# A two-layer hybrid trunk on one Trainium2 core: one block of scores for both key triangles of sliding attention, and running sums by four products

## The chip, the cores and the metric

The kernel runs on one core of a Trainium2 chip. The metric is the device time of one execution in microseconds (us), and lower is better. A core has five engines that matter here: TensorE (PE in the profile; its weight loads are PEld), VectorE (DVE), ScalarE (ACT), GpSimd (POOL) and SyncE (SP). Each works through its own instructions in the order in which the program holds them, and waits for others through semaphores. On-chip data lies in SBUF, products of TensorE in PSUM, inputs and outputs in DRAM.

## What is computed

Two layers, each applied to a stream of 256 tokens of width 1024. A layer projects the normalised stream by one large matrix, feeds three token mixers (a state-space scan called SSD, sliding-window attention, and "forgetting" attention with a decay bias), gates and projects each, merges them, projects once more and adds to the stream. The parts that the change touches are these, cut from the reference:

```
# sliding attention: 16 heads of 64, 4 key/value heads, window 128, blocks of 128 queries
scores = einsum(qb, kb) * 64**-0.5                  # kb: the block before and the own block, 256 keys
diff = qi + 128 - sj                                # 0 <= diff < 128 is inside the window
scores = where(0 <= diff < 128 and key_pos >= 0, scores, -inf)
probs = softmax(concat([scores, sink]))[..., :-1]   # the sink takes a share and has no value
y = einsum(probs, vb) * silu(z)
# forgetting attention
log_f = log_sigmoid(f_logit + f_bias);  cum = cumsum(log_f, axis=1)      # over all 256 tokens
sc = sc + cum[query] - cum[key]
# SSD: decays inside a chunk of 128 tokens
a_cum = cumsum(dt * a)                              # per chunk;  decay = exp(a_cum[l] - a_cum[s])
```

For the second block of queries, the inside of the window is a triangle of the previous block's keys (key index above the query's) and the complementary triangle of the own block's keys (key index at or below the query's). Together they have 128 keys per query.

## The kernel before

**Dense work and weights.** All weights come from DRAM in parts of 512 KB (`load_part`, issued on SP's queue). Each part is split into two: `hi`, a copy on ScalarE (L291), and `lo`, the rest, on VectorE (L292, `lo = raw - hi`). A dense product takes three products, hi by hi and two with a `lo`. Six buffers hold raw parts and six hold split parts; a split buffer is released when TensorE has used it.

**The order of TensorE's work** is written by a planner while the program is built. `mm` and `transpose` (L100 to L110) put an instruction on TensorE and move a planned clock on. The mixers are generators: one is `launch`ed, and when it yields a number (the constants D_..., L25 to L27) it is asked again once the planned clock has moved on by so many microseconds. `pump` (L147) enters those that are due after each dense unit. So TensorE's order is fixed by hand, and dense products lie between the steps of a mixer. The orders of VectorE, ScalarE and GpSimd are set by the tile scheduler when the program is built.

**PSUM** has eight banks of 128 by 512: `pmm` gives three in turn to dense products, `pmx` gives five in turn to everything else. A bank that is given out again is written only after its last reader is done.

**Sliding attention** takes four heads at a time (a "quad", four quads per layer; `swa_quad` and `attn_quad`, L587 to L687). A quad takes four `pmx` banks for the scores of its four heads: 128 columns for the first block of queries (own keys) and 256 for the second (previous and own keys). TensorE fills them by 32 products. VectorE adds the mask and takes the row minimum (L615, once per block and head: 128 and 256 wide, into SBUF), ScalarE takes the exponential with its row sum (L621), a few small operations add the sink's share (L625 to L628), then come a reciprocal (L630) and eight scalings (L633). After D_SOFT = 7 planned microseconds TensorE transposes twelve 128 by 128 blocks (L647) in two halves, D_SOFT2 = 3 apart; ScalarE copies the three resulting banks to SBUF (L652). After D_EVAC = 3 come the products with the values. Two quads' values are taken together, at the start of a later quad (L676: gate times product, on VectorE, straight from PSUM). `attn_quad` also serves forgetting attention.

**Running sums** (`decay_logits`, L714 to L763): from 32 logits per token a chain of small VectorE operations makes the rates of the SSD (`da`) and of the forgetting (`lf`). D_CUM = 12 planned microseconds after that, TensorE makes the sums by products with a triangle of ones: two into a bank `pa` (tokens on the partitions, evicted to `acum`), two into a bank `pr` (heads on the partitions, SSD) and three into a bank `pf` (heads on the partitions, forgetting). `pr` and `pf` go through ScalarE to one SBUF tile and by one DMA to DRAM (`cumd`, L763), from where each group of SSD heads (L808) and each pair of forgetting heads (L985) reads its rows, copied to all 128 partitions.

In TensorE's order the sums of a layer stand after the scores of its third sliding quad. Of the five `pmx` banks, four are then that quad's scores; `pa` takes the fifth, `pr` the bank of its first head, `pf` the bank of its second.

Of the kernel before, what the change touches and what calls it, by code (L numbers as in the profile page):

```python
# [16 lines left out]
P = 128  # L17
# [30 lines left out]
def hybrid_trunk(  # L48
# [29 lines left out]
    def pmx():  # L78
        return PS("mx", 5)
# [105 lines left out]
    for j in range(2):  # L185
# [16 lines left out]

    wmask = T("wmask", [P, 2 * P])
    nc.gpsimd.memset(wmask, 0.0)
    nc.gpsimd.affine_select(out=wmask[:, P:2 * P], in_=wmask[:, P:2 * P],
                            compare_op=ALU.is_ge, fill=NEG, base=0,
                            pattern=[[-1, P]], channel_multiplier=1)
    nc.gpsimd.affine_select(out=wmask[:, 0:P], in_=wmask[:, 0:P],
                            compare_op=ALU.is_ge, fill=NEG, base=-1,
                            pattern=[[1, P]], channel_multiplier=-1)  # L210
    mhalf = T("mhalf", [P, 8])
# [374 lines left out]

    def attn_quad(y, last, products, biases, nsink, v, vcols, sz, gated, scored=lambda: None):  # L587

# [18 lines left out]
        products(score)  # L607
        for p in range(2):
            pp = pps[p]
            ps_ = slice(4 * p, 4 * p + 4)  # L610
            ns = None if nsink is None else nsink(p)
            for i in range(2):
                for b, sl in blocks:
                    e = 4 * p + 2 * i + b
                    nc.vector.tensor_tensor_reduce(  # L615
                        out=pp[:, i, sl], in0=score(p, i, b), in1=biases(p, i, b), scale=-0.125,
                        scalar=1.0e30 if ns is None else ns[:, i:i + 1],
                        op0=ALU.add, op1=ALU.min, accum_out=nm[:, e:e + 1])
                for b, sl in blocks:
                    e = 4 * p + 2 * i + b  # L620
                    act(pp[:, i, sl], pp[:, i, sl], AF.Exp, scale=-1.0, bias=nm[:, e:e + 1],  # L621
                        accum_out=sums[:, e:e + 1])
            if nsink is not None:
                es = T("es", [P, 4], bufs=2)
                tt(es.rearrange("p (i b) -> p i b", i=2), nm[:, ps_].rearrange("p (i b) -> p i b", i=2),  # L625
                   bc(ns, 2, 2), op=ALU.subtract)
                act(es, es, AF.Exp)
                tt(sums[:, ps_], sums[:, ps_], es, op=ALU.add)  # L628
            rs = T("rsum", [P, 4], bufs=4)
            nc.vector.reciprocal(rs, sums[:, ps_])  # L630
            for i in range(2):
                for b, sl in blocks:
                    ts(pp[:, i, sl], pp[:, i, sl], rs[:, 2 * i + b:2 * i + b + 1], 0.5,  # L633
                       op0=ALU.mult, op1=ALU.mult)
        yield D_SOFT
        scored()

        order = [(0, 0), (0, 1), (1, 0), (1, 1), (0, 2), (1, 2),
                 (2, 0), (2, 1), (2, 2), (3, 0), (3, 1), (3, 2)]
        at = {hb: (n // 4, n % 4 * P) for n, hb in enumerate(order)}  # L640
        pTs = []
        for n, (h, b) in enumerate(order):
            if n == 6:
                yield D_SOFT2
            if n % 4 == 0:
                pt = pmx()
            transpose(pt[:, n % 4 * P:(n % 4 + 1) * P], pps[h // 2][:, h % 2, b * P:(b + 1) * P], ident)  # L647
            if n % 4 == 3:
                if n == 3:
                    two = T("L4", [P, 2, 512])  # L650
                pT = T("L2", [P, 512]) if n == 11 else two[:, n // 4, :]
                act(pT, pt, AF.Copy)  # L652
                pTs.append(pT)
        yield D_EVAC
        tokens["pp"] += 1

        def products_with_values(bank):
            py = bank()
            for p in range(2):
                for b, o in ((0, 0), (1, P)):  # L660
                    for i in range(2):
                        n, c = at[2 * p + i, 2 * b]
                        mm(py[64 * i:64 * i + 64, S * p + o:S * p + S], v[:, b, vcols(p, i)],
                           pTs[n][:, c:c + S - o], start=(b == 0), stop=(b == 1))
            return py
# [3 lines left out]
        if len(pair) == 2:  # L669
# [3 lines left out]
            def values():  # L673
                for py, (_, _, own) in zip([f(bank) for (_, f, _), bank in zip(quads, (pmx, pmm))], quads):
                    o = own()
                    tt(o, py.rearrange("p (u s) -> p u s", u=2), o, op=ALU.mult)  # L676
            if not last:
# [8 lines left out]
    def swa_quad(y, g, q):  # L686
        yield lambda: 1 in y.sz  # L687

        def products(score):
# [7 lines left out]
        yield from attn_quad(  # L697
            y, g == 3, products, lambda p, i, b: wmask[:, P:2 * P] if b == 0 else wmask,
            lambda p: y.nsink[:, 4 * g + 2 * p:4 * g + 2 * p + 2], y.bv,
            lambda p, i: slice(64 * g, 64 * g + 64),  # L700
            lambda: y.sz[1][:, 2 * g:2 * g + 2, :], lambda: (1, 2 * g + 1) in y.zdone)

# [11 lines left out]
    def decay_logits(y):  # L714
# [20 lines left out]
        y.dt = T("dt", [P, 2, 16])  # L735
        lf = T("lf", [P, 2, 16])
        ts(w[:, :, 0:16], u[:, :, 0:16], 0.0, 0.5, op0=ALU.max, op1=ALU.mult)
# [3 lines left out]
        tt(lf, w[:, :, 16:32], q3[:, :, 16:32], op=ALU.subtract)  # L741
        ts(lf, lf, 2.0, None, op0=ALU.mult)
        da = T("da", [P, 2, 16])
        tt(da, y.dt, bc(y.nega, 1, 2), op=ALU.mult)
# [7 lines left out]
        cum = T("L2", [16, 2, S])  # L752
# [225 lines left out]
    def fox_quad(y, j):  # L978
# [535 lines left out]
```

## Time and profile before

| | us |
|---|---|
| median of 3 runs | 820.61 (819.9 to 821.44) |
| the profiled execution | 820.72 |
| its span in the trace | 819.0 |
| PE busy in it | 808.4 |
| DVE busy | 671.5 |
| ACT busy | 547.6 |
| POOL busy | 172.6 |

The profiled execution's time is 1.72 us above its span: that much lies around the first and last instruction that the trace shows. A page of the profile gives busy times of the engines, the granted TensorE clock (PEclk), a chain of waits that ended last, and groups of instructions by source line. A timeline row gives start, duration, engine, line, operation, output and inputs, shape and count. Most durations overlap the next instruction's start, since engines are pipelined: what an instruction costs its engine's queue is the distance from its start to the next one's.

### The profile page before, as it was taken

How to read it: one execution, taken by the hardware profiler on the slowest of the kernel's cores; microseconds unless marked ns; L12 is line 12 of the kernel's file. 1: busy time of each engine (PE TensorE's matmuls, PEld its weight loads, DVE VectorE, ACT ScalarE, POOL GpSimd, SP SyncE). 2: the span in 40 equal slices, each digit the busy share in tenths (PEclk: the TensorE clock that was granted, in tenths of full speed). 3: DMA queues.
4: the chain of work that ended last, by engine and by line, in shares of the span. 5: the costliest groups of instructions: out<-in, count | busy, mean ns of one | idle time of the engine just before them, and what ended most of it. 6: DMA issues, size and time to landing. Idle time of an engine off the chain costs nothing.

```text
span 819.0 us, 15070 instructions
## 1 busy us (share of the span) xinstructions
PE 808.4 (99%) x5242; PEld 721.2 (88%) x5242; DVE 671.5 (82%) x1468; ACT 547.6 (67%) x1186; POOL 172.6 (21%) x232
## 2 busy tenths in 40 slices
PE   8999999999999999999999999999999999999996
PEld 8998988888888988888999898889888889888896
DVE  6879899888998787965786989988899878787665
ACT  7777878775776767543666777886567767684452
POOL 3066113130210001030005621314004210102100
PEclk9999999999999999999999999999999999999999
DMA  9897869797865554866689787869868565467632
GB/s 312 278 261 193 211 187 256 190 233 214 232 206 157 180 168 148 276 208 205 221 265 265 186 222 206 228 179 259 243 206 231 155 181 163 137 208 265 206 104 77
DMA packets 141653, 170.35 MB, mean 208 GB/s; under 512 B 9314, under 2 KB 110298, under 8 KB 141578
## 3 DMA queue, kind: packets, MB, share of 16 engines
q1 hardware_dynamic: 114960, 140.53, 54.8%
q0 software_dynamic: 12928, 12.63, 9.5%
q10 hardware_dynamic: 13690, 16.24, 6.5%
q8 instruction: 41, 0.67, 0.3%
q14 instruction: 34, 0.28, 0.1%
HBM read 154.63 MB, written 2.16 MB: 191 GB/s over the span
## 4 chain that ended last, share of the span: by engine, by line
PE 85%; DVE 4%; DMA 4%; ACT 4%; issue 2%; POOL 0%; SPq 0%; ACTq 0%; DVEq 0%; POOLq 0%
PE mm L106 75%; PE mx L106 7%; PE mx L110 3%; DMA L<-cumd 2%; DVE lo L292 1%; ACT hi L291 1%; DVE L L781 1%; ACT pp L621 1%; DMA L<-L 1%; DMA raw<-in_w_in_dram 1%; DMA bias<-cumd 1%; ACT L L778 0%; ACT L L490 0%; DVE L L830 0%; POOL bias L991 0%
## 5 line engine op out<-in xcount | busy, mean ns | idle before, releaser
L292 DVE TENSOR_TENSOR lo<-raw,hi 128x1024 fp32r<-128x1024 f32 (+2 forms) x276 | 310.5, 1144 | 53.2 <-ACT hi L291 50.5
L106 PE MATMUL mm<-L,hi 128*128 128x512 f32 x1056 | 353.2, 386 | 0.0
L106 PE MATMUL mm<-hi,L 128*128 128x512 f32 (+2 forms) x1232 | 323.3, 351 | 0.1
L291 ACT ACTIVATE hi<-raw 128x1024 fp32r<-128x1024 f32 (+2 forms) x276 | 263.9, 981 | 57.2 <-PE mm L106 45.2
L106 PE MATMUL mm<-L,lo 128*128 128x256 f32 x1056 | 266.6, 273 | 0.0
L106 PEld LDWEIGHTS mm<-hi,L 128*128 128x128 f32 x1232 | 216.9, 190 | 24.1 <-issue 1.3
L106 PEld LDWEIGHTS mm<-L,hi 128*128 128x128 f32 x1056 | 194.5, 190 | 26.4 <-issue 3.2
L106 PE MATMUL mm<-lo,L 128*128 128x512 f32 (+2 forms) x616 | 213.8, 349 | 1.8 <-DVE lo L292 1.8
L106 PEld LDWEIGHTS mm<-L,lo 128*128 128x128 f32 x1056 | 202.1, 191 | 5.5
L106 PEld LDWEIGHTS mm<-lo,L 128*128 128x128 f32 x616 | 116.3, 190 | 14.1 <-DVE lo L292 2.6
L492 POOL DMA_DIRECT2D L<-L x68 | 59.4, 925 | 184.5 <-ACT L L491 151.3
L621 ACT ACTIVATE pp<-pp,nm 128x128 f32<-128x128 f32 (+1 forms) x128 | 56.5, 442 | 30.8 <-DVE nm L615 30.7
L991 POOL TENSOR_SCALAR_AFFINE_SELECT bias<-bias 128x128 f32<-128x128 f32 x64 | 34.6, 592 | 93.5 <-DMA bias<-cumd 92.7
L781 DVE SCALAR_TENSOR_TENSOR L<-L,vec,L 128x255 f32<-128x255 f32 (+2 forms) x96 | 46.2, 481 | 2.2 <-ACT L L778 0.5
L490 ACT ACTIVATE L<-mm 128x256 f32<-128x256 f32 x84 | 31.6, 376 | 15.9 <-PE mm L106 14.2
L1025 ACT ACTIVATE L<-L 128x512 f32<-128x512 f32 x24 | 15.1, 629 | 31.6 <-DVE L L1022 27.2
L633 DVE TENSOR_SCALAR pp<-pp,rsum 128x128 f32<-128x128 f32 (+1 forms) x128 | 32.5, 319 | 0.5
L492 POOL DMA_DIRECT2D qt<-L x16 | 14.5, 990 | 81.9 <-ACT qt L491 40.4
L877 DVE SCALAR_TENSOR_TENSOR L<-L,L 128x256 f32<-128x256 f32 x48 | 21.4, 449 | 8.6 <-ACT L L876 8.3
L652 ACT ACTIVATE L<-mx 128x512 f32<-128x512 f32 x48 | 26.8, 595 | 1.5 <-PE mx L110 1.5
L1070 POOL TENSOR_TENSOR L<-L,L 128x512 f32<-128x512 f32 x8 | 12.8, 1598 | 68.4 <-DVE L L1069 68.4
L912 POOL TENSOR_TENSOR sm<-sm,mhalf 128x4 f32<-128x4 f32 x8 | 8.1, 1019 | 90.5 <-DVE sm L909 90.5
(197 smaller groups left out, 841.8 us busy)
## 6 DMA issues: line engine op xcount, KB each, us to landing
raw<-in_w_in_dram SPq DMA_DIRECT2D x191, 512.0 KB, 4.7
raw<-in_w_proj_dram SPq DMA_DIRECT2D x48, 512.0 KB, 5.3
L<-L POOLq DMA_DIRECT2D x72, 128.0 KB, 5.0
raw<-in_w_out_dram SPq DMA_DIRECT2D x16, 512.0 KB, 5.1
bias<-cumd ACTq DMA_DIRECT2D x16, 256.0 KB, 3.4
L<-cumd ACTq DMA_DIRECT2D x8, 512.0 KB, 5.9
L<-in_gate_bias_dram ACTq DMA_DIRECT2D x12, 256.0 KB, 5.9
qt<-L POOLq DMA_DIRECT2D x16, 128.0 KB, 5.6
```

The lines of the kernel that those rows point to most:

```text
L106: nc.tensor.matmul(o, a, b, **kw)
L110: nc.tensor.transpose(o, a, i)
L291: keep(act)(hi, src, AF.Copy)
L292: keep(tt)(lo, src, hi.bitcast(F32), op=ALU.subtract)
L490: act(halves(lo), ordered(p[:, S:2 * S]), AF.Copy)
L492: nc.gpsimd.dma_start(out, lo, accum_op=ALU.add)
L621: act(pp[:, i, sl], pp[:, i, sl], AF.Exp, scale=-1.0, bias=nm[:, e:e + 1], accum_out=sums[:, e:e + 1])
L633: ts(pp[:, i, sl], pp[:, i, sl], rs[:, 2 * i + b:2 * i + b + 1], 0.5, op0=ALU.mult, op1=ALU.mult)
L652: act(pT, pt, AF.Copy)
L781: stt(a[:, s:S], x_[:, 0:S - s], y.vec[:, 16 * j + u:16 * j + u + 1], a[:, s:S], op0=ALU.mult, op1=ALU.add)
L877: stt(o, th, 1.0, o, op0=ALU.add, op1=ALU.mult)
L991: nc.gpsimd.affine_select(out=bias[:, i, dst], in_=bias[:, i, src], compare_op=ALU.is_ge, fill=NEG, base=0, pattern=[[-1, P]], channel_mul ...
```

## The change

Sliding attention (`window=True`) and the running sums are rewritten; forgetting attention keeps its code.

- **One block of scores.** The first block of queries is treated as before. In the second block, the previous block's scores are copied over the own block's scores wherever the own ones are masked, by a predicated copy inside PSUM, once per head. The 128 wide result gets its row maximum by a reduction, a small operation per two heads makes the bias, and ScalarE's exponential reads PSUM itself, 128 wide in place of 256.
- **Normalisation** by two operations per quad (128 by 512, reciprocals broadcast) in place of eight scalings. The factor 0.5 goes to the gate's operation after the values.
- **Transposes.** Eight per quad in place of twelve. The first half's bank is copied by ScalarE; the second half's bank is taken twice by VectorE, times the mask `other` and times the triangle `tri`, to part the two triangles again. The first half is asked for after D_FOLD = 8 in place of D_SOFT = 7.
- **Running sums.** Both rates share a tile; `pa` takes one product, and a bank `pc` takes three (two chunks in column groups, with 32 columns for both rates, and one that adds the first chunk's total to the forgetting sums). One copy of 64 by 128 goes to SBUF and two DMAs write `cumd`, now `[2, 16, 256]`, so that the later readers' rows lie side by side. D_CUM is 17 in place of 12.

```
-D_GN1, D_GN2, D_CUM, D_H, D_M = 8.0, 13.5, 12.0, (4.8, 6.4), 5.0
+D_GN1, D_GN2, D_CUM, D_H, D_M = 8.0, 13.5, 17.0, (4.8, 6.4), 5.0
+D_FOLD = 8.0
...
+        def chances(h, b, of):
+            e = 4 * b + h
+            act(pps[b][:, h // 2, h % 2 * P:h % 2 * P + P], of, AF.Exp, scale=0.125 if b else -1.0,
+                bias=nm[:, e:e + 1], accum_out=sums[:, e:e + 1])
+
+        for h in range(4) if window else ():
+            own = pps[0][:, h // 2, h % 2 * P:h % 2 * P + P]
+            nc.vector.tensor_tensor_reduce(
+                out=own, in0=scs[h][:, 0:P], in1=wmask, scale=-0.125, scalar=nsink[:, h:h + 1],
+                op0=ALU.add, op1=ALU.min, accum_out=nm[:, h:h + 1])
+            chances(h, 0, own)
+        for h in range(4) if window else ():
+            own = scs[h][:, 2 * P:3 * P]
+            nc.vector.copy_predicated(own, wmask.bitcast(mybir.dt.uint32), scs[h][:, P:2 * P])
+            nc.vector.tensor_reduce(nm[:, 4 + h:5 + h], own, axis=mybir.AxisListType.X, op=ALU.max)
+            if h % 2 == 1:
+                hs = slice(h - 1, h + 1)
+                nh = slice(3 + h, 5 + h)
+                stt(nm[:, nh], nm[:, nh], -0.125, nsink[:, hs], op0=ALU.mult, op1=ALU.min)
+                for i in (h - 1, h):
+                    chances(i, 1, scs[i][:, 2 * P:3 * P])
+        for b in range(2) if window else ():
+            ...
+            nc.vector.reciprocal(rs, sums[:, hs])
+            tt(of_heads(b), of_heads(b), bc(rs.rearrange("p (i j) -> p i j", i=2), 3, P), op=ALU.mult)
...
-        yield D_SOFT
+        yield D_FOLD if window else D_SOFT
...
+                for h in range(4):
+                    transpose(pt[:, h * P:(h + 1) * P], pps[b][:, h // 2, h % 2 * P:h % 2 * P + P], ident)
+                ptv = pt.rearrange("p (h q) -> p h q", h=4)
+                if b == 0:
+                    act(first[:, 0, :], pt, AF.Copy)
+                else:
+                    tt(first[:, 1, :].rearrange("p (h q) -> p h q", h=4), ptv, bc(other, 1, 4), op=ALU.mult)
+                    tt(both.rearrange("p (h q) -> p h q", h=4), ptv, bc(tri, 1, 4), op=ALU.mult)
...
+                    if window:
+                        stt(o, po, 0.5, o, op0=ALU.mult, op1=ALU.mult)
...
         yield D_CUM
         pa = pmx()
-        for c in range(2):
-            mm(pa[:, 16 * c:16 * c + 16], tri, da[:, c, :], start=True, stop=True)
+        mm(pa[:, 0:32], tri, rates[:, :, 1, :], start=True, stop=True)
...
-        pr = pmx()
+        pc = pmx()
         for c in range(2):
-            mm(pr[0:16, c * P:(c + 1) * P], da[:, c, :], tri, start=True, stop=True)
-        act(cum[:, 0, :], pr[0:16, 0:S], AF.Copy)
-        pf = pmx()
-        mm(pf[0:16, 0:P], lf[:, 0, :], tri, start=True, stop=True)
-        mm(pf[0:16, P:S], lf[:, 0, :], ones, start=True, stop=False)
-        mm(pf[0:16, P:S], lf[:, 1, :], tri, start=False, stop=True)
-        act(cum[:, 1, :], pf[0:16, 0:S], AF.Copy, scale=-8.0)
-        y.cumd = dr.tile([16, 2, S], F32, name=f"cumd{y.l}", tag=f"cumd{y.l}")
-        nc.scalar.dma_start(y.cumd, cum)
+            mm(pc[32 - 32 * c:64 - 32 * c, 0:P], rates[:, c, :, :].rearrange("p w c -> p (w c)"), tri,
+               start=True, stop=(c == 0))
+        mm(pc[0:16, 0:P], rates[:, 0, 0, :], ones, start=False, stop=True)
+        cum = T("L1", [64, P])
+        act(cum, pc[0:64, 0:P], AF.Copy)
+        y.cumd = dr.tile([2, 16, S], F32, name=f"cumd{y.l}", tag=f"cumd{y.l}")
+        for c in range(2):
+            nc.scalar.dma_start(y.cumd[:, :, c * P:(c + 1) * P].rearrange("w c s -> (w c) s"),
+                                cum[32 - 32 * c:64 - 32 * c, :])
...
-        nc.scalar.dma_start(bcg, y.cumd[4 * g:4 * g + 4, 0, :].partition_broadcast(P))
+        nc.scalar.dma_start(bcg, y.cumd[1, 4 * g:4 * g + 4, :].partition_broadcast(P))
...
-                                y.cumd[2 * (j + p):2 * (j + p) + 2, 1, :].partition_broadcast(P))
+                                y.cumd[0, 2 * (j + p):2 * (j + p) + 2, :].partition_broadcast(P))
```

In the changed program, too, a layer's sums stand after the scores of the third sliding quad, sixteen dense instructions behind them; `pa` has the fifth bank and `pc` the bank of that quad's first head, whose second block ScalarE's exponential now reads.

More of the change, by code (lines that the diff above doesn't have):

```diff
@@ L585, in u_bq, with attn_quad @@
         return rotated(y, done)
-    def attn_quad(y, last, products, biases, nsink, v, vcols, sz, gated, scored=lambda: None):
+    def attn_quad(y, last, products, biases, nsink, v, vcols, sz, gated, scored=lambda: None, window=False):
         yield Half("pp")
@@ L607, in attn_quad, with of_heads @@
         products(score)
-        for p in range(2):
+        def of_heads(b):
+            return pps[b].rearrange("p i (j q) -> p i j q", j=3)[:, :, 0:2, :]
+        def chances(h, b, of):
[19 more added lines that the diff above has]
+        for b in range(2) if window else ():
+            hs = slice(4 * b, 4 * b + 4)
+            es = T("es", [P, 4], bufs=2)
+            tt(es, nm[:, hs], nsink, op=ALU.subtract)
+            act(es, es, AF.Exp)
+            tt(sums[:, hs], sums[:, hs], es, op=ALU.add)
+            rs = T("rsum", [P, 4], bufs=4)
+            nc.vector.reciprocal(rs, sums[:, hs])
+            tt(of_heads(b), of_heads(b), bc(rs.rearrange("p (i j) -> p i j", i=2), 3, P), op=ALU.mult)
+        for p in () if window else range(2):
             pp = pps[p]
             ps_ = slice(4 * p, 4 * p + 4)
-            ns = None if nsink is None else nsink(p)
             for i in range(2):
@@ L661, in products_with_values @@
                     for i in range(2):
[L662 to L664 removed]
+                        h = 2 * p + i
+                        if window:
+                            m = both[:, h * P:(h + 1) * P] if b else first[:, :, h * P:(h + 1) * P]
+                        else:
+                            n, c = at[h, 2 * b]
+                            m = pTs[n][:, c:c + S - o]
+                        mm(py[64 * i:64 * i + 64, S * p + o:S * p + S], v[:, b, vcols(p, i)], m,
+                           start=(b == 0), stop=(b == 1))
             return py
@@ L697, in swa_quad @@
         yield from attn_quad(
-            y, g == 3, products, lambda p, i, b: wmask[:, P:2 * P] if b == 0 else wmask,
-            lambda p: y.nsink[:, 4 * g + 2 * p:4 * g + 2 * p + 2], y.bv,
+            y, g == 3, products, None, y.nsink[:, 4 * g:4 * g + 4], y.bv,
             lambda p, i: slice(64 * g, 64 * g + 64),
-            lambda: y.sz[1][:, 2 * g:2 * g + 2, :], lambda: (1, 2 * g + 1) in y.zdone)
+            lambda: y.sz[1][:, 2 * g:2 * g + 2, :], lambda: (1, 2 * g + 1) in y.zdone, window=True)
     def logits(y, t, i, p):
```

69 lines of the change are left out of this document (35 added, 34 removed).

## The prediction

> **What bounds the kernel now.** I read the page first: busy times, granted clock and the chain that ended last.
>
> ```profile
> span 819.0 us, 15070 instructions
> PE 808.4 (99%) x5242; PEld 721.2 (88%) x5242; DVE 671.5 (82%) x1468; ACT 547.6 (67%) x1186; POOL 172.6 (21%) x232
> PEclk9999999999999999999999999999999999999999
> PE 85%; DVE 4%; DMA 4%; ACT 4%; issue 2%; POOL 0%; SPq 0%; ACTq 0%; DVEq 0%; POOLq 0%
> ```
>
> TensorE is busy for 99% of the span at the full clock, and 85% of the chain is its own. VectorE at 82% is next. Then the waits of PE (total, times, longest), and the two stretches that hold the sliding quads, one per layer (length, busy time of PE, PEld, DVE, ACT, POOL, clock, DMA share):
>
> ```profile
> PE mm L106 <- DVE lo L292: 1.8, 2, 1.2
> 66.00:160.00 94.00, 94.00 (x723) 84.02 (x722) 86.19 (x236) 75.89 (x202) 27.65 (x34) 1.00 0.75 200
> 457.00:552.00 95.00, 94.82 (x726) 84.51 (x726) 86.50 (x237) 75.93 (x202) 27.50 (x34) 1.00 0.74 199
> ```
>
> In both stretches PE has no idle time worth a name, and DVE is busy for 86.2 of 94 and 86.5 of 95 us, 91 to 92%. So an instruction taken from PE saves its time, as long as PE then waits for nobody; but DVE, which the change touches most, has only some 8 us of slack in 94. Over the whole kernel PE waits 1.8 us for late `lo` parts, in two waits.
>
> **Work taken from PE.** The chain of waits through layer 0's quads (start, length, what) gives the price of one instruction:
>
> ```profile
> 75.97 0.66 PE mx L110 x6
> 112.53 1.52 PE mx L106 x32
> 114.06 2.82 PE mm L106 x16
> 116.88 1.54 PE mx L106 x14
> ```
>
> Six transposes take 0.66 us, 0.11 each. The change drops 4 of 12 per quad, 8 quads: 32 x 0.11 = 3.5 us. The seven products of the running sums (14 records, two passes each) take 1.54 us, 0.22 each; four remain, so 3 x 0.22 x 2 layers = 1.3 us. **PE's own work: -4.8 us.** The score products, the products with values and all dense work stay.
>
> **A wait that goes.** In layer 1 the old sums already waited a little:
>
> ```profile
> 116.71 0.51 PE L106 MATMUL mx<-da,tri 128*128 128x16 f32 x4
> 117.16 0.61 PE L106 MATMUL mx<-tri,da 128*16 128x128 f32 x4
> 507.97 0.52 PE L106 MATMUL mx<-da,tri 128*128 128x16 f32 x4
> 508.60 0.61 PE L106 MATMUL mx<-tri,da 128*16 128x128 f32 x4
> 509.28 0.39 PE L106 MATMUL mx<-tri,lf 128*16 128x128 f32 x2
> ```
>
> `pa` to `pr` is 0.45 us in layer 0 and 0.63 in layer 1, `pr` to `pf` 0.68 where four records at 0.11 need 0.44. That is about 0.4 us of waiting for the banks of the quad's heads. Those products go: **-0.4**. What is late next is the following term.
>
> **A wait that comes: `pc` on the bank of the third quad's first head.** `pr` got that bank when VectorE had read it (L615 writes to SBUF, so its last reader is the second L615 row of that head). Now the bank is held through predicated copy, reduction, the small operation for two heads, and ScalarE's exponential, which reads PSUM. PE stands still at `pc`, and all dense work queues behind it. So I compare two arrival times in layer 0.
>
> *PE at `pc`.* Counted with the prices above through the changed order, the third quad's scores come 1.7 us later than now (more dense work and the later D_FOLD lie ahead; fewer transposes). They end at 112.53 + 1.52 + 1.7 = 115.75. Then stand sixteen dense instructions (2.82) and `pa` (0.22): PE is at `pc` at 118.8.
>
> *VectorE at the quad.* Its timeline now:
>
> ```profile
> 102.47 2.36 DVE L292 TENSOR_TENSOR lo<-raw,hi 128x1024 fp32r<-128x1024 f32 x2 [0.75 <-ACT hi L291]
> 104.75 0.48 DVE L781 SCALAR_TENSOR_TENSOR L<-L,vec,L 128x255 f32<-128x255 f32 x1
> 105.14 0.17 DVE L709 TENSOR_TENSOR u<-mm,hb 128x16 f32<-128x16 f32 x1
> ...
> 114.01 0.68 DVE L676 TENSOR_TENSOR L<-mx,L 128x512 f32<-128x512 f32 x1
> 114.61 0.21 DVE L733 SCALAR_TENSOR_TENSOR L<-L 128x64 f32<-128x64 f32 x1
> ...
> 116.01 0.34 DVE L615 CUSTOM_DVE_ANT_0 pp<-mx,wmask,nsink 128x128 f32<-128x128 f32 x1
> 116.28 0.48 DVE L615 CUSTOM_DVE_ANT_0 pp<-mx,wmask,nsink 128x256 f32<-128x256 f32 x1
> 116.68 0.35 DVE L615 CUSTOM_DVE_ANT_0 pp<-mx,wmask,nsink 128x128 f32<-128x128 f32 x1
> ```
>
> The last idle time is the 0.75 us ahead of 102.47. From there the queue runs without a gap for 13.54 us to the quad's first row at 116.01, although the scores were there at 114.05: DVE is already 1.95 us behind. That stretch, from the same `lo` to the same row, holds 5 `lo`, 6 filter taps (L781) and the sums' chain. In the changed order it holds 7 `lo`, 9 taps, and the two new mask products of the second quad. A `lo` takes 2.36/2 = 1.14 to 1.18 of the queue, a tap 0.39 (104.75 to 105.14), a 128 by 512 product from PSUM 0.60 (114.01 to 114.61): 2 x 1.14 + 3 x 0.39 + 2 x 0.60 = 4.7 us more, 18.2 in all. Because less lies ahead on DVE and PE, I let the stretch start 0.3 to 1.6 us sooner; the quad's first row is then at 102.47 - 0.3 (1.6) + 18.2 = 120.4 (119.1).
>
> *Time to free the bank.* Behind that first row DVE's order has three more 128 wide mins, three predicated copies, three reductions and the small operation before head 0's exponential. A min takes 0.27 of the queue (116.01 to 116.28). No row shows the predicated copy or a 128 wide reduction. From below stand a small reduction and an all-SBUF operation of 128, from above the min at twice the width:
>
> ```profile
> L246 DVE TENSOR_REDUCE sm<-ss 128x1 f32<-128x2 f32 x4 | 0.6, 148 | 0.8 <-ACT L L242 0.8
> 179.47 2.19 DVE L830 SCALAR_TENSOR_TENSOR L<-L,acum,negtri 128x128 f32<-128x128 f32 x8
> L621 ACT ACTIVATE pp<-pp,nm 128x128 f32<-128x128 f32 x64 | 24.9, 390 | 30.5 <-DVE nm L615 30.5
> ```
>
> That is 0.15 to 0.40 for a reduction and 0.27 (2.19/8) to 0.40 for a copy; I take 0.25 and 0.27, those of like width. Then 4 x 0.27 + 3 x 0.27 + 3 x 0.25 + 0.1 = 2.75 us (2.4 to 3.5). The exponential takes 0.39, and two hand-overs between engines some 0.25. The bank is free 3.4 us after the first row, at 122.5 to 123.8, and PE has waited since 118.8: **3.7 to 5.0, I take 4.3 us in layer 0.** In layer 1 the queue is further behind:
>
> ```profile
> 503.73 1.59 PE L106 MATMUL mx<-L,qt 32*128 32x128 f32 x32
> 507.79 0.34 DVE L615 CUSTOM_DVE_ANT_0 pp<-mx,wmask,nsink 128x128 f32<-128x128 f32 x1
> ```
>
> Scores from 503.73 end by 505.25, the first row is at 507.79: 2.54 behind, against 1.95. So **4.9 in layer 1, 9.2 together.** D_CUM = 17 in place of 12 does not help: the planner's clock asks for the sums right behind this quad's scores either way.
>
> **The rest of DVE's and ACT's work.** Per quad the rows below change (count, busy total and mean in ns, idle before):
>
> ```profile
> L615 DVE CUSTOM_DVE_ANT_0 pp<-mx,wmask,nsink 128x256 f32<-128x256 f32 x32 | 15.2, 476 | 0.0
> L633 DVE TENSOR_SCALAR pp<-pp,rsum 128x256 f32<-128x256 f32 x64 | 22.5, 352 | 0.0
> L633 DVE TENSOR_SCALAR pp<-pp,rsum 128x128 f32<-128x128 f32 x64 | 18.4, 287 | 0.5
> L652 ACT ACTIVATE L<-mx 128x512 f32<-128x512 f32 x48 | 26.8, 595 | 1.5 <-PE mx L110 1.5
> L621 ACT ACTIVATE pp<-pp,nm 128x256 f32<-128x256 f32 x64 | 31.7, 495 | 0.2 <-DVE nm L615 0.2
> ```
>
> DVE loses four mins of 256 (1.6) and the scalings (about 2.2) and gains four copies, four reductions, two wide normalisations and two mask products (1.1 + 1.0 + 1.2 + 1.2), and two small operations: about +1 us a quad. ACT loses two copies of 0.6 and gets four narrower exponentials. Off the places named, this lies beside PE's dense work. If the cover is thin, it is at the second quad's first transposes, whose normalisation now waits for all four heads: 0 to 0.4 us a layer, **+0.3 in all**. The gate's factor 0.5 rides on an operation that exists. The mask products have D_EVAC and the next quad between them and the values; cost nothing, and 1.2 us a quad if DVE were the bound there.
>
> **Transfers.** The `cumd` tile is now written by two DMAs and read in longer rows. Its readers stand in the chain that leads to the late `lo`:
>
> ```profile
> 159.47 8.88 DMA L<-cumd
> 168.58 4.83 DMA bias<-cumd
> ...
> 182.93 1.14 DVE lo L292
> ```
>
> PE waits 1.8 us behind such chains. Reads with rows of 4 and 2 KB in place of 1 KB may be shorter, or no different: 0 to -1.8, **I take -1.0**. The write is off the chain: the first reader asks for it some 40 us after the sums.
>
> **The sum**, against the profiled execution's 820.72 (0.11 above the median of the runs, 820.61): -4.8 - 0.4 + 9.2 + 0.3 - 1.0 = +3.3, so **824.0 us**.
>
> **Rivals.**
> - *The clock drops in the wait.* The waits of 4 to 5 us would be the longest of PE in the kernel after its start. How PE runs after idling is seen at the start only:
>
> ```profile
> 1.52 1.76 PE L110 MATMUL mx<-ident 128*128 128x128 f32 x7 [1.52 <-POOL ident masks.py:199]
> 5.38 1.38 PE L110 MATMUL mx<-ident 128*128 128x128 f32 x10
> ```
>
>   Seven transposes at 1.52 took 1.76/7 = 0.25 each, ten at 5.38 took 0.14, where 0.11 is the price later on: for some 4 us PE ran at about half speed. If each wait of over 3 us brings such a stretch back, 1.7 to 3.4 us are lost per layer: 826 to 831 us. Against it: the clock is 1.00 in both stretches, and waits up to 1.2 us did not touch it. The Trainium skill, "TensorE: Matmul & The Clock Gate", Part 1 (The HAM clock gate), says that one idle window of about 3.4 us, counted by a free-running window, puts the clock back to half; by that rule a wait of 4.3 us would sometimes be enough, with this rival's time, and sometimes not; no run here shows it.
> - *The wait is about half as long* (2.1 to 3.7 us a layer), since `lo` splits that stand ahead of the quad are released sooner with PE's work gone: 819.0 to 822.3.
> - *The other side: VectorE is not behind.* Without any wait at `pc` the sum is 820.72 - 4.8 - 0.4 + 0.3 - 1.0 = 814.8. From there each us of wait per layer costs 2 us, so the change gains as long as the wait stays under 2.95 us a layer, and shows as a gain under 2.1: 814.8 to 819.0. That needs VectorE's queue to reach the third quad 1.6 us or more sooner than the earliest I find. For it: the 8 us of slack in 94, which an earlier idle of 0.75 shows to be not all used up. Against it: the gap-free 13.54 us and the two `lo` and three taps that moved ahead.
> - *The reads of `cumd` shorten nothing, the rest as forecast*: 825.0, inside the forecast's range.
>
> **How the numbers follow.** Forecast (wait of 3.7 to 5.5 us a layer, 822.3 to 826): 0.48. Clock drops, 826 to 831: 0.17. Half the wait, 819.0 to 822.3: 0.17. VectorE not behind, 814.8 to 819.0: 0.18. A measurement of this kernel can tell about 0.2%, 1.6 us, from no change; so faster 0.18, same 0.17, slower 0.65. The range 817.0 to 828.5 leaves out the lower half of the last case (0.09) and the upper half of the clock's (0.08). A predicated copy and a reduction at 0.40 each would add 0.8 us a layer and stay inside it.
>
> **What would show it.** In the changed profile: PE's waits should name the exponential (ACT, in the bank of `pc`) twice with 4 to 5 us, PE's transposes of `pp` should be 160, and DVE's first min of the third quad should start 3.4 us or more behind the last score. The clock's row must be read behind both waits. The prediction is wrong if PE goes through the sums without a wait, or if a wait of equal size appears at another place: at the transposes (normalisation), the values (mask products) or a `lo`.

## The result, and the profile after

The changed kernel takes **824.58 us** (median of 4 runs, 824.13 to 826.03), the kernel before 820.66 (4 runs); the ratio is 1.0051, 95% interval 1.0033 to 1.0068. It is slower by half a per cent. The forecast was 824.0. The profiled execution of the change took 824.13, its span 822.3.

Four lines of the page of the change, the same that were shown of before:

```profile
span 822.3 us, 14971 instructions
PE 806.2 (98%) x5198; PEld 719.4 (87%) x5198; DVE 675.8 (82%) x1452; ACT 539.6 (66%) x1168; POOL 163.6 (20%) x233
PEclk9999999999999999999999999999999999999999
PE 90%; DVE 6%; ACT 2%; issue 1%; DMA 0%; ACTq 0%; DVEq 0%
```

PE is busy for 2.2 us less, and yet the span is 3.3 us longer: PE now waits. The waits of PE in the change, and the two stretches with the sliding quads:

```profile
PE mx L107 <- ACT pp L614: 8.0, 2, 4.0
66.00:160.00 94.00, 89.98 (x667) 80.58 (x667) 87.20 (x226) 69.93 (x189) 25.08 (x34) 0.98 0.76 201
457.00:552.00 95.00, 90.97 (x673) 81.39 (x672) 87.40 (x224) 70.22 (x192) 25.53 (x34) 0.98 0.76 202
```

Two waits of 4.0 us, one per layer, for L614, the exponential; the waits for late `lo` parts (L292) are gone from the list. The clock column shows 0.98 where it was 1.00.

A table by stage says where the 3.3 us came from. Stages run from one milestone on PE to the next: the first score product of the layer's sliding quads 1, 3 and 4, the first score product of forgetting attention (fox), and the last product of all. In us:

| stage | before | change | sums later (D_CUM = 23) |
|---|---|---|---|
| start to quad 1, layer 0 | 66.3 | 66.2 | 66.5 |
| quad 1 to 3, layer 0 | 46.1 | 47.9 | 47.9 |
| quad 3 to 4, layer 0 | 23.1 | 27.6 | 21.8 |
| quad 4 to fox, layer 0 | 76.4 | 74.6 | 76.9 |
| fox to quad 1, layer 1 | 245.6 | 243.0 | 243.0 |
| quad 1 to 3, layer 1 | 46.1 | 47.9 | 47.9 |
| quad 3 to 4, layer 1 | 23.5 | 27.5 | 21.8 |
| quad 4 to fox, layer 1 | 88.3 | 84.4 | 87.1 |
| fox to the end | 197.1 | 197.1 | 197.1 |

The planner moves 1.7 us of dense work from the later stages ahead of quad 3; that nets out. The loss stands between quads 3 and 4, where the running sums are: 4.4 and 4.0 us. The last column is an experiment, told below.

The wait itself, PE's timeline of the change (the scores of the third quad, `pa`, `pc`, and two dense products behind it):

```profile
114.12 1.59 PE L107 MATMUL mx<-L,qt 32*128 32x128 f32 x32
118.36 0.30 PE L107 MATMUL mx<-rates,tri 128*128 128x32 f32 x2
122.69 0.41 PE L107 MATMUL mx<-tri,rates 128*32 128x128 f32 x4 [4.02 <-ACT pp L614]
...
124.06 0.64 PE L107 MATMUL mm<-L,hi 128*128 128x512 f32 x1
124.49 0.42 PE L107 MATMUL mm<-L,lo 128*128 128x256 f32 x1
...
127.09 0.38 PE L107 MATMUL mm<-L,hi 128*128 128x512 f32 x1
127.31 0.27 PE L107 MATMUL mm<-L,lo 128*128 128x256 f32 x1
```

VectorE and then ScalarE over the same time:

```profile
118.41 1.21 DVE L292 TENSOR_TENSOR lo<-raw,hi 128x1024 fp32r<-128x1024 f32 x1
119.54 0.34 DVE L619 CUSTOM_DVE_ANT_0 pp<-mx,wmask,nsink 128x128 f32<-128x128 f32 x1
...
121.14 0.48 DVE L627 COPY_PREDICATED mx<-wmask,mx 128x128 f32<-128x128 uint32 x2
121.54 0.48 DVE L628 TENSOR_REDUCE nm<-mx 128x1 f32<-128x128 f32 x2
121.94 0.15 DVE L632 SCALAR_TENSOR_TENSOR nm<-nm,nsink 128x2 f32<-128x2 f32 x1
```

```profile
119.92 0.40 ACT L614 ACTIVATE pp<-pp,nm 128x128 f32<-128x128 f32 x1 [6.36 <-DVE nm L619]
...
122.18 0.37 ACT L614 ACTIVATE pp<-mx,nm 128x128 f32<-128x128 f32 x1 [0.40 <-DVE nm L632]
```

The scores end at 114.12 + 1.52 = 115.64. VectorE finishes a `lo` first and comes to the quad at 119.54, 3.9 us behind. ScalarE has stood idle for 6.36 us ahead of its first exponential. The exponential that reads head 0's second block starts at 122.18, and with its end PE gets the bank at 122.69. Behind the wait a dense product of 512 takes 124.49 - 124.06 = 0.43 us of PE, and from 127.09 on 0.22: PE has run at half speed for some 3.4 us. The granted clock shows it (stretch, length, busy PE, PEld, DVE, ACT, POOL, clock):

```profile
122.50:126.00 3.50, 3.31 (x16) 2.72 (x17) 3.15 (x12) 2.94 (x16) 0.86 (x1) 0.64 0.06 21
126.00:129.50 3.50, 3.50 (x20) 3.19 (x20) 2.85 (x5) 2.72 (x6) 0.71 (x1) 0.87 0.33 49
129.50:133.00 3.50, 3.50 (x25) 3.21 (x24) 1.75 (x3) 2.79 (x6) 1.01 (x2) 1.00 0.91 221
```

Over the first two stretches the clock lacks 0.36 and 0.13 of 3.5 us, together 1.7 us, which is 3.4 us at half clock. So each layer pays twice, 4.0 us of waiting and, since the stage without either takes 21.76 us, 27.56 - 21.76 - 4.02 = 1.8 us for the clock; 1.8 in layer 1 too. The page's row of clock digits does not show this: a slice there is 20 us long.

### The profile page after: what moved, and what is told of

Same layout as the page of the kernel before. It is cut to its first block, busy times and chain, and to the rows that moved or that the text cites. A ratio compares the mean times of both kernels' runs of the same rounds, so it can differ in the third digit from the quotient of the medians.

```text
span 822.3 us, 14971 instructions
## 1 busy us (share of the span) xinstructions
PE 806.2 (98%) x5198; PEld 719.4 (87%) x5198; DVE 675.8 (82%) x1452; ACT 539.6 (66%) x1168; POOL 163.6 (20%) x233
## 4 chain that ended last, share of the span: by engine, by line
PE 90%; DVE 6%; ACT 2%; issue 1%; DMA 0%; ACTq 0%; DVEq 0%
PE mm L107 80%; PE mx L107 7%; PE mx L111 4%; DVE lo L292 2%; DVE L L833 2%; ACT pp L614 1%; ACT hi L291 0%; DVE pp L619 0%; DMA L<-in_x_dram 0%; DVE pp L643 0%; DVE L L784 0%; DVE mx L627 0%; DVE L L727 0%; DVE L L840 0%; DVE L L680 0%
## 5 line engine op out<-in xcount | busy, mean ns | idle before, releaser
L107 PE MATMUL mm<-L,hi 128*128 128x512 f32 x1056 | 357.0, 389 | 0.0
L292 DVE TENSOR_TENSOR lo<-raw,hi 128x1024 fp32r<-128x1024 f32 (+2 forms) x276 | 312.0, 1149 | 53.8 <-ACT hi L291 50.9
L490 ACT ACTIVATE L<-mm 128x256 f32<-128x256 f32 x84 | 31.9, 379 | 25.9 <-PE mm L107 22.8
L1043 POOL TENSOR_SCALAR_AFFINE_SELECT bias<-bias 128x128 f32<-128x128 f32 x64 | 28.1, 476 | 87.4 <-DMA bias<-cumd 60.6
L1077 ACT ACTIVATE L<-L 128x512 f32<-128x512 f32 x24 | 15.1, 629 | 30.4 <-DVE L L1074 25.9
L656 ACT ACTIVATE pp<-pp,nm 128x128 f32<-128x128 f32 x64 | 28.2, 442 | 9.9 <-DVE nm L650 9.9
L614 ACT ACTIVATE pp<-pp,nm 128x128 f32<-128x128 f32 x32 | 12.6, 393 | 24.9 <-DVE nm L619 24.1
L964 POOL TENSOR_TENSOR sm<-sm,mhalf 128x4 f32<-128x4 f32 x8 | 9.9, 1241 | 88.0 <-DVE sm L961 88.0
L491 ACT ACTIVATE L<-mm 128x256 f32<-128x256 f32 x68 | 25.9, 380 | 1.0 <-DMA L<-L 1.0
L928 ACT ACTIVATE L<-L 128x256 f32<-128x256 f32 x48 | 19.8, 413 | 9.3 <-DVE L L483 9.1
```

What stands on the lines that cost most here:

```text
L107: nc.tensor.matmul(o, a, b, **kw)
L292: keep(tt)(lo, src, hi.bitcast(F32), op=ALU.subtract)
L490: act(halves(lo), ordered(p[:, S:2 * S]), AF.Copy)
L491: last = act(halves(out), ordered(p[:, 0:S]), AF.Copy)
L614: act(pps[b][:, h // 2, h % 2 * P:h % 2 * P + P], of, AF.Exp, scale=0.125 if b else -1.0, bias=nm[:, e:e + 1], accum_out=sums[:, e:e + 1])
L928: act(th, o, AF.Tanh, scale=0.5)
```

## The experiments

Theory: PE waits at `pc` because the bank of the third quad's first head is held until an exponential that hangs on a late VectorE; the clock drops because of the wait. Rivals: VectorE is late as such, so PE will wait elsewhere when the sums are moved; the new sums bring the wait and not the fold; the slow stretch has a cause of its own. All ratios are to the kernel before, with its runs on the same chip, 95% interval in brackets.

**The sums later: D_CUM = 21**

```
-D_GN1, D_GN2, D_CUM, D_H, D_M = 8.0, 13.5, 17.0, (4.8, 6.4), 5.0
+D_GN1, D_GN2, D_CUM, D_H, D_M = 8.0, 13.5, 21.0, (4.8, 6.4), 5.0
```

> The change with D_CUM = 21 in place of 17: the sums of a layer stand 31 instead of 16 dense instructions behind the third quad's scores, 2.6 us later on PE; nothing else moves. Theory (PE waits at pc for a bank that the late exponential holds, 4.0 us a layer, and the clock is low for some 3.5 us behind it): the wait shrinks to 1.4 us a layer and the clock stays at 1.00, time 824.6 - 2 x 2.6 - 3.2 = 816 us. Rival (VectorE is late for the quad whatever waits on it, PE stands at the quad's transposes instead): 822 to 824.6, with PE waits at L111. Rival on the clock (any wait behind an idle engine lowers it): waits of 1.4 us and still some 3 us lost, 819.

Measured: 821.96 us, 1.0014 (1.0004 to 1.0023). PE's waits, and the row of `pc`:

```profile
PE mx L107 <- ACT pp L614: 2.8, 2, 1.4
PE mm L107 <- DVE L L1074: 2.4, 2, 1.3
```

```profile
122.55 0.41 PE L107 MATMUL mx<-tri,rates 128*32 128x128 f32 x4 [1.40 <-ACT pp L614]
```

The wait is 1.4 us as worked out, and the clock stays at 1.00. But the time is some 6 us above the forecast of 816. The stage from quad 3 to 4 gained its 4.3 us per layer; the next one, up to fox, lost 2.7 and 3.1, with a new wait for a gate's sum (L1074).

**The sums later still: D_CUM = 23** (the same line with 23.0)

> D_CUM = 23: the sums stand 46 dense instructions behind the third quad's scores, some 5 us later than with 17, right ahead of its first transposes. Theory (bank held): no wait at pc, no drop of the clock, 824.6 - 8.0 - 3.2 = 813.4 us, all PE waits in the quads under 0.5 us. Rival (VectorE late as such): the waits reappear at the transposes, 820 to 824.

Measured: **818.76 us, 0.9974 (0.9962 to 0.9986)**: faster than both kernels. No wait at `pc`, none at the quad's transposes; the rows follow each other:

```profile
123.84 0.30 PE L107 MATMUL mx<-rates,tri 128*128 128x32 f32 x2
124.07 0.41 PE L107 MATMUL mx<-tri,rates 128*32 128x128 f32 x4
...
124.64 0.66 PE L111 MATMUL mx<-ident,pp 128*128 128x128 f32 x4
```

In the table above, the stage from quad 3 to 4 falls by 5.8 us per layer, wait and clock together. Of these 11.6 us, 5.0 are given back between quad 4 and fox (2.3 and 2.7). The rival was wrong on the place, and right in that part of the time is lost again: not at the third quad, but in a later stage, when PE no longer stands still. The largest of its waits:

```profile
PE mm L107 <- DVE L L1074: 2.2, 2, 1.2
```

**The two parts of the change apart.** The running sums alone, in the kernel before (`decay_logits` and the two reads of `cumd` from the change, D_CUM = 12):

```
+        mm(pa[:, 0:32], tri, rates[:, :, 1, :], start=True, stop=True)
...
+        pc = pmx()
```

> The kernel before with the change's running sums alone (rates in one tile, four products, two writes of cumd, readers with longer rows), D_CUM = 12 and the old sliding attention. Theory: six fewer products in all, 1.3 us, and 0.2 to 0.4 of waiting at the sums, and no wait at pc because L615 frees the bank: 819.0 us. If the longer rows also shorten the chain to the two late lo parts: 817 to 818, with PE's waits for L292 under 1 us in all. Rival (the sums in their new form bring the wait, not the fold): 822 or more.

Measured: 820.22 us, 0.9992 (0.9984 to 1.0001). PE's waits:

```profile
PE mx L106 <- DVE nm L615: 1.2, 2, 0.8
PE mm L106 <- DVE lo L292: 1.0, 2, 0.6
```

The forecast of no wait at `pc` failed: PE waits 0.4 us in layer 0 and 0.8 in layer 1, for L615 on VectorE, and most of what the three products saved goes into it: PE comes to the bank sooner and VectorE doesn't. The rival, 822 or more, fell too.

The fold alone: the change with the old `decay_logits` and the old layout of `cumd`.

```
-        pc = pmx()
+        pr = pmx()
...
+        pf = pmx()
```

> The change with the old seven products, three banks and one write of cumd, sliding attention in its new form, sums at the same place. Theory: PE waits at pr 3.8 us a layer for the same exponential, the clock drops behind it, and 0.44 us a layer of products are added: 825.5 us. If the shorter rows of cumd bring back the late lo: 826.5 to 827.5. Rival (the new sums bring the wait): 816 to 818.

Measured: 827.04 us, 1.0070 (1.0058 to 1.0082).

```profile
123.13 1.03 PE L107 MATMUL mx<-tri,da 128*16 128x128 f32 x4 [3.81 <-ACT pp L614]
```

The wait of 3.8 us is there with the old sums: the fold brings it. The seven products now stand in the slow stretch (1.03 us for the first four records, before 0.61), which makes the old sums dearer. In layer 0 the clock stays at half for 6.8 us in place of 3.4, and the stage from quad 3 to 4 takes 29.3 us (in the change 27.6; in layer 1 28.2 against 27.5). No wait for a late `lo` is left, with the old short rows of `cumd`. So the time lies in the range that was forecast for late `lo` parts, but by luck: the slow stretches made it.

**Another bank for `pc`**

```
-        pc = pmx()
+        pc = pmm()
```

> The change with one edit: pc takes its bank from the three dense banks (pmm) in place of the five others, so that no exponential holds it; the sums stay at their place (D_CUM = 17). The rates are ready on VectorE (row at 116.32) before PE comes to the sums (118.36). Theory (the bank, not the data, is waited for): no wait at pc, clock 1.00, and the time of the sums set later (818.8), 818 to 820. Rival (PE needs something else that late VectorE makes): the wait of 4 us a layer stays or appears at the quad's transposes, 822 to 825.

Measured: 820.34 us, 0.9988 (0.9978 to 0.9997). PE's timeline:

```profile
119.51 0.41 PE L107 MATMUL mm<-tri,rates 128*32 128x128 f32 x4
...
125.38 0.48 PE L107 MATMUL mm<-L,hi 128*128 128x512 f32 x1 [2.42 <-ACT L L491]
```

`pc` goes without a wait: it was the bank, not the data. But now three dense banks also serve `pc`, and 2.4 us of the wait come back one dense unit later, for an eviction (L491) on ScalarE. ScalarE works in order and stood behind the same exponentials. In the profiled execution (822.31, the slowest of 11) both waits were followed by a slow stretch; the clock of one:

```profile
124.00:127.50 3.50, 2.12 (x8) 1.91 (x9) 3.27 (x10) 3.50 (x13) 0.86 (x1) 0.77 0.14 21
```

The 11 runs spread from 818.4 to 822.3 us, with mean granted clocks from 0.998, as in kernels without a drop, down to 0.994, as in the change with its two: after 2.4 us the clock seems to drop in some executions and not in others. Only the profiled one has a trace.

**Extra work in the wait.** Twelve (and six) extra products whose result nobody uses, first put between `pa` and `pc`:

```
+        for _ in range(12):
+            nc.tensor.matmul(pa[:, S:S + P], tri, tri, start=True, stop=True)
         pc = pmx()
```

> The change with twelve extra products of 128x128 per layer between pa and pc, triangle by triangle into unused columns of pa's bank; their result is not used. They take 12 x 0.22 = 2.6 us of the 4.0 us in which PE idles, so PE's idle time is 1.4. Theory (the clock drops because PE idles for some 4 us): clock 1.00 behind the sums, 1.8 us a layer saved, minus what is given back later: 821 to 823. Rival (the slow stretch behind the wait has another cause, such as the restart of dense work or late weights): the rows behind pc keep 0.43 us a product and the time stays at 824 to 825.

> As before with six extra products: 1.3 us of the wait filled, 2.7 us idle. If the clock drops only for idle times of over 3 us or so: clock 1.00, 821 to 823. If 2.7 us are enough: 824 to 825 and a slow stretch of some 3.5 us behind pc in both layers.

Measured: 837.54 us, 1.0194 (1.0181 to 1.0208), and 834.30, 1.0155 (1.0141 to 1.0168). Both tests missed their aim. The extra products write the bank that ScalarE's copy to `acum` reads, and that copy stands behind the exponentials in ScalarE's order:

```profile
125.11 5.28 PE L806 MATMUL mx<-tri 128*128 128x128 f32 x23 [6.69 <-ACT acum L802]
```

PE waited 6.7 us in place of 4.0, although the columns don't overlap. On the clock they say only that it drops after such a wait too: 23 records in 5.28 us are 0.23 each, twice the 0.11 of the full clock.

So the products were put ahead of `pa`:

```
+        for _ in range(12):
+            nc.tensor.matmul(pa[:, S:S + P], tri, tri, start=True, stop=True)
         mm(pa[:, 0:32], tri, rates[:, :, 1, :], start=True, stop=True)
```

> The change with twelve extra products of 128x128 per layer ahead of pa's product, into unused columns of its bank; pa's only reader comes later, so they wait for nobody. Result not used. They take 2.6 us, so PE comes to pc at 121.2 and idles 1.4 us instead of 4.0. Theory (the clock drops because PE idles for long; a wait of 1.4 us with the sums set later left it at full speed): clock 1.00 behind pc, the stretch from the third to the fourth quad's scores 25.8 us instead of 27.5, 1.8 us a layer saved, 821 to 822 us. Rival (the slow stretch has another cause): 27.5 us and 824 to 825.

> The same with six extra products, 1.3 us: PE idles 2.7 us. With pc in a dense bank a wait of 2.4 us was followed by 2.0 us lost. If 2.7 us are enough to lower the clock: stretch of 27.5 us or more, 824 to 825. If not: 25.8, 821 to 822.

Measured: twelve, 821.65 us, 0.9998 (0.9989 to 1.0007); six, 824.89, 1.0034 (1.0021 to 1.0047). With twelve, the rows of PE and the clock behind `pc`:

```profile
118.61 2.84 PE L801 MATMUL mx<-tri 128*128 128x128 f32 x24
...
122.93 0.41 PE L107 MATMUL mx<-tri,rates 128*32 128x128 f32 x4 [1.33 <-ACT pp L614]
```

```profile
123.00:126.50 3.50, 3.50 (x24) 3.04 (x25) 3.19 (x11) 2.67 (x14) 0.86 (x1) 1.00 0.05 9
```

With six:

```profile
123.27 0.45 PE L107 MATMUL mx<-tri,rates 128*32 128x128 f32 x4 [2.68 <-ACT pp L614]
```

```profile
123.00:126.50 3.50, 3.23 (x14) 2.53 (x15) 3.19 (x11) 3.01 (x16) 0.86 (x1) 0.57 0.09 30
```

Counted from the first quad's first score product (66.23, 66.48 and 66.81 us in the change, with twelve and with six), PE gets the bank at the same time in all three kernels, after 56.5 us. With twelve useless products, 1.3 us of idle time and full clock, the stage from quad 3 to 4 takes 25.9 us in both layers, 1.6 to 1.7 less than in the change, and the ratio to before is 0.9998 where that of the change is 1.0051. With six and 2.7 us of idle time the clock drops, and the time is that of the change. So the idle time sets the slow stretch.

The traces also show which part of an idle time counts. Narrow stretches of the profile give the edges of the clock, and in every trace they lie whole steps of 3.41 us behind its first rise near the start: in the change it rises at 7.45, is at half from 123.50 (34 steps later) to 126.91, and again from 516.03 (149 steps) to 519.45. While TensorE had work, a step that held 2.0 us or more of its idle time was always followed by a drop, and one that held 1.4 us or less never was. A wait of 2.25 us, in a kernel further below (the normalisation on ScalarE, layer 0), is parted by the end of a step into 1.36 and 0.89 us, and the clock stays; one of 2.47 us in its layer 1 lies inside a step, and the clock drops. Where the wait falls among the steps can so differ from run to run, which fits the spread of the 11 runs above; it isn't shown for them.

The Trainium skill, "TensorE: Matmul & The Clock Gate", Part 1 (The HAM clock gate), has the clock back at half after an idle window of about 3.4 us. The step of 3.41 us agrees in length, but it need not be idle as a whole: here 2.7 us were enough in both layers of the profiled execution, 2.4 us in both layers of one execution with `pc` in a dense bank, and 1.4 us were not. The measurement decides, and a margin below the stated figure is needed.

**What holds back the stage after quad 4.** With D_CUM = 23, the rows ahead of the gate's sum on VectorE, on ScalarE, and PE behind it:

```profile
148.09 3.50 DVE L292 TENSOR_TENSOR lo<-raw,hi 128x1024 fp32r<-128x1024 f32 x3
151.50 0.68 DVE L1074 TENSOR_TENSOR L<-mm,L 128x512 f32<-128x512 f32 x1
```

```profile
147.00 3.89 ACT L291 ACTIVATE hi<-raw 128x1024 fp32r<-128x1024 f32 x4
```

```profile
152.34 0.46 PE L107 MATMUL mm<-L,hi 128*128 128x512 f32 x1 [0.98 <-DVE L L1074]
```

VectorE has no idle time there from 132 us on, so I took its queue for the bound, and took work from it in three ways. One mask product per quad less (the first mask product replaced by a copy on ScalarE, since the two triangles' products with values v1 and v0 are those of the whole block with v0 and of one triangle with v1 - v0):

```
-                    tt(first[:, 1, :]..., ptv, bc(other, 1, 4), op=ALU.mult)
+                    act(first[:, 1, :], pt, AF.Copy)
...
+                gtt(y.dv, y.bv[:, 1, :], y.bv[:, 0, :], op=ALU.subtract)
```

> D_CUM = 23, and one mask product per quad leaves VectorE: ScalarE copies the second half's bank whole (0.6 us), the triangle's share meets the difference of the two blocks of values (made once per layer by GpSimd), so only the product with tri stays on VectorE: 0.6 us less per quad. With D_CUM = 23 PE waits 1.2 us a layer for a gate's sum on VectorE (L1074) and the stretch from the fourth quad to forgetting attention is 2.3 to 2.7 us longer than in the change. Theory (VectorE's queue is the next bound there): that stretch gets 1 to 2 us shorter per layer, 815 to 817.5 us. Rival (the stretch is bound by the reads of cumd or by ScalarE): 818.5 to 820.

Measured: 819.64 us, 0.9980 (0.9971 to 0.9989), no better than D_CUM = 23 without it (0.9974). In its profiled execution (817.82, the fastest of 12) the stretch from quad 4 to fox is 0.6 us longer in layer 0 and 1.2 us shorter in layer 1. In layer 0, VectorE spent what it saved waiting for ScalarE's new copy (L684 of this kernel):

```profile
136.77 0.69 DVE L685 TENSOR_TENSOR L<-mx,tri 128x512 f32<-128x512 f32 x1 [0.96 <-ACT L L684]
```

The fourth quad's normalisation left out, and the same on ScalarE:

```
+            if not last:
                 tt(of_heads(b), of_heads(b), bc(...), op=ALU.mult)
```

> D_CUM = 23 with the normalisation of each layer's fourth quad left out (two products of 128x512 on VectorE, 1.2 us per layer). VectorE has no idle time from 136 us to the gate's sum (L1074 in the change), for which PE then waits 1.2 us. Theory (that gap-free queue is what bounds PE there): the wait goes, 1.1 us a layer, and the stretch from the fourth quad to forgetting attention takes some 75.7 instead of 76.9 us: 816 to 817 us. Rival (ScalarE, the transfers or the bank rotation bound it): the wait stays over 0.8 us, 818 to 819.

```
+            for h in range(4) if last else ():
+                o = pps[b][:, h // 2, h % 2 * P:h % 2 * P + P]
+                act(o, o, AF.Copy, scale=rs[:, h:h + 1])
```

> D_CUM = 23 with the fourth quad's normalisation on ScalarE, eight copies with a scale per token of about 0.28 us each, in place of 1.2 us on VectorE. Theory: VectorE's queue is shorter as above, ScalarE has 70 of 94 us in use and takes 2.2 us: 816 to 818 us. Rival (ScalarE's queue, which makes the hi parts and the gates' tanh, becomes the bound): 818.8 to 821.

Measured: left out, 819.47 us, 0.9970 (0.9958 to 0.9982), the same as with it; on ScalarE, 821.07, 0.9993 (0.9984 to 1.0002). The rows of the first: VectorE now idles, and PE waits all the same.

```profile
147.53 0.43 DVE L930 SCALAR_TENSOR_TENSOR L<-L,L 128x256 f32<-128x256 f32 x1 [0.61 <-ACT L L929]
148.49 3.50 DVE L292 TENSOR_TENSOR lo<-raw,hi 128x1024 fp32r<-128x1024 f32 x3 [0.53 <-PE mx L111]
```

```profile
152.73 0.45 PE L107 MATMUL mm<-L,hi 128*128 128x512 f32 x1 [1.31 <-DVE L L1075]
```

The second row starts as soon as the first of ScalarE's four `hi` is done, at 148.45, although the profile names TensorE for the wait. With the eight copies on ScalarE, the wait doubles:

```profile
154.12 0.45 PE L107 MATMUL mm<-L,hi 128*128 128x512 f32 x1 [2.25 <-DVE L L1078]
```

In layer 1 it is 2.47 us, and there the clock drops behind it, which is part of the 2.3 us by which this kernel is slower than that with D_CUM = 23:

```profile
543.00:546.50 3.50, 1.59 (x8) 1.47 (x9) 3.50 (x5) 3.31 (x7) 0.00 (x0) 0.89 0.59 174
546.50:549.00 2.50, 2.50 (x10) 2.13 (x8) 2.46 (x4) 2.35 (x3) 0.86 (x1) 0.50 1.02 354
```

So VectorE's queue alone is not the bound there: that theory fell. 1.2 us of normalisation taken from it change nothing, and the eight copies put on ScalarE add 1.3 us to the wait. What fits these rows, without being shown, is a path through both: the quad's exponentials on ScalarE, then four `hi` splits behind them, then three `lo` on VectorE, each behind its `hi`, and the gate's sum behind these in VectorE's order. That the sum's place behind the three `lo` is what counts was not tried. Of the 2.3 and 2.7 us of the stage, the wait for the gate's sum explains 1.0 and 1.2. PE has the same instructions in the same order there as in the change, so the rest can be placed row by row: with D_CUM = 23 it loses 0.2 us more right behind the gate's sum, 0.3 at 169 us in layer 0 and at the same place in layer 1, 0.5 at 175 us (0.7 in layer 1) behind an eviction on ScalarE (L491), and 0.3 at 193 us (0.2 in layer 1). Only a quarter to a third of that is idle time; what slows PE otherwise stays open.

## Why the prediction was right, step by step

- **PE's work, -4.8.** The 160 transposes are there, and PE's busy time fell by 2.2 us although the clock's stretches added 3.6; without these it would have fallen by 5.8, a little more than forecast.
- **The wait at `pc`, 9.2.** Right in its mechanism, and 8.0 in size (4.0 and 4.0 for 4.3 and 4.9). The milestones in layer 0: PE at `pc` at 118.8, measured 122.69 - 4.02 = 118.67; the quad's first min at 119.1 to 120.4, measured 119.54; the bank free at 122.5 to 123.8, measured 122.69. Copy and reduction take 0.20 us of the queue each (121.14 to 121.54 for two), not 0.27 and 0.25. For layer 1 I added 0.6 because VectorE was further behind there before; in the change it is not.
- **The clock.** I gave it as a rival with 0.17. It did drop, in both layers, for 1.8 us each, the lower end of the 1.7 to 3.4 of that rival. That the time was still the forecast's and not the rival's 826 to 831 is because other terms were too high: the waits by 1.2, PE's work by 1.0, and the next two steps. The mechanism of the largest term held; that 824.0 came within 0.6 us of the measured time, with a drop of the clock left out of the sum, is luck.
- **The late `lo`, -1.0.** It was -1.8, and the reason failed. Reads of `cumd` did not get shorter (median from issue to landing, change):

```profile
bias<-cumd ACTq DMA_DIRECT2D x16, 256.0 KB, 3.5
L<-cumd ACTq DMA_DIRECT2D x8, 512.0 KB, 5.8
```

  Before they were 3.4 and 5.9. The fold with the old rows has no late `lo` either, and the sums alone, with the new rows, still wait 1.0 us for it. The waits go with the fold. With D_CUM = 23 they are gone too, so the new wait at `pc` isn't what removes them; by which part of the fold they go stays open.
- **The waits of the old sums, -0.4, and the transposes, +0.3.** The first went with the old products; the second didn't come: no wait at L111 for `pp` is in the list.
- **Sum with the measured sizes**: waits +8.0, clock +3.6, PE's work -4.8, late `lo` -1.8, old sums -0.4 make +4.6; the spans differ by 3.3. The missing 1.3 us are mostly the 1.0 by which PE's busy time fell further than I counted.
- **"From there each us of wait costs 2 us"** and "without any wait 814.8": this rival's arithmetic failed. Without a wait at `pc` the kernel takes 818.8, since the stage after quad 4 holds back 5 us as soon as PE is earlier.

## What to carry to other kernels

An operation that reads PSUM in place of SBUF lengthens the life of its bank by the whole queue ahead of it on every engine in its chain: look up in the order who gets that bank next, and compare when each arrives. A wait on TensorE is not priced by its length alone: here 2.4 us and more could take the clock with it, 1.4 us did not, and then even useless products in the gap were a gain (821.65 us against 824.58); setting the consumer later needs no extra work and gave more (818.76). And what a removed wait returns is bounded by the next engine in line: here 11.6 us went at one place and 5.0 came back at another.

## What the runs showed of the hardware

- Idle times of TensorE of 1.3 to 1.4 us left the granted clock at 1.00, and so did one of 2.25 us; in the traces it dropped after each of 2.4, 2.5, 2.7, 3.8, 4.0 and 6.7 us. Its edges lay at whole steps of 3.41 us from its first rise; 2.0 us or more of idle time inside one step brought a drop, 1.4 us or less did not.
- A drop lasted one step and cost 1.8 us in the change. It lasted two or three steps, 6.8 or 10.2 us, where TensorE idled 0.6 us or more in a slow step too (the fold alone in layer 0, the extra products behind `pa`).
- A predicated copy inside PSUM of 128 by 128 takes 0.20 us of VectorE's queue, and so does a row maximum of 128 from PSUM (busy 290 and 285 ns each):

```profile
L627 DVE COPY_PREDICATED mx<-wmask,mx 128x128 f32<-128x128 uint32 x32 | 8.6, 290 | 0.3
L628 DVE TENSOR_REDUCE nm<-mx 128x1 f32<-128x128 f32 x32 | 8.5, 285 | 0.0
```

- Products into columns of a PSUM bank that nobody reads waited 6.7 us for the reader of other columns of the same bank. The wait stands in the program, as a semaphore; no run shows whether the chip would need it.
